# An attention stage whose projections, scores and value products yield more often to each other

## The chip, the cores and the metric

The program runs on one core of one Trainium2 chip. Five engines work side by side, each through its own list of instructions in a fixed order: TensorE (PE, matrix products; PEld is its weight load), VectorE (DVE), ScalarE (ACT), GpSimd (POOL) and SyncE (SP), which here issues nearly all of the transfers. The metric is device time in microseconds (us). The kernel before took 1922.65 us, the median of three runs (1921.36 to 1924.04).

## The reference

One step of a two-layer backbone runs over 128 context tokens and 512 latent tokens, 1024 wide. Layer 0 is softmax attention, layer 1 a gated delta rule; each is followed by an MLP of width 4096. The change touches layer 0's attention alone: 8 query heads of 128, 2 key/value heads. Cut to what it computes:

```python
proj = h @ w_in                                  # query, key and value columns
q, k = rms_norm(q, q_gain), rms_norm(k, k_gain)  # per head
q, k = axial_rope(q, ang), axial_rope(k, ang)    # latent tokens alone
s = einsum('bqkgd,bskd->bkgqs', q, k) * HEAD_DIM ** -0.5
o = einsum('bkgqs,bskd->bqkgd', softmax(s), v)   # latent queries see cached + latent keys
```

Context queries see context keys alone.

## The kernel before, in words

Activations lie as 128 features by 640 tokens, one tile per block of 128 features. Every fp32 matrix is split into a high and a low part (`split`: ScalarE copies the high part, another engine subtracts it), and one product is three matmuls (`mm3`: high by high, high by low, low by high).

A head passes three generators. `attn_proj` loads the head's weights (one transfer of 512 KB by SP; ScalarE makes the high part, GpSimd the low one), projects 320 tokens and then the other 320 (24 matmuls each, into one PSUM tile each; ScalarE copies the result and squares it), sums the squares by 10 short matmuls, and turns the query: four transfers on SP's queue fetch its quarters exchanged, GpSimd multiplies twice, VectorE adds, and the result is split again. `attn_scores` makes 24 score matmuls for four blocks of 128 latent queries and 3 for the context block; per block VectorE takes the maximum, ScalarE the exponential with its sum, VectorE the reciprocal, and GpSimd scales. `attn_values` transposes the four blocks' probabilities for one tile of keys (4 matmuls), ScalarE and VectorE split the result, and 3 matmuls add it to the output; this five times, then once for the context block.

What sets the order: `weave` runs generators in turns. It always advances the one whose next step has the smallest (steps done + 1) / weight. The loop at the end of `attention` runs eight rounds; round n weaves the value product of head n, the scores of head n+1 and the projection of head n+2. Before it, one weave holds keys, values and the query of head 0 (`attn_kv`, which ends with a projection of its own) beside eight loads of `w_mod` (`modulate`, two transfers of 512 KB each), and a second one the scores of head 0 beside the projection of head 1. The order that the generators give is a priority; a scheduler then lists each engine's instructions, and may put a ready one ahead of one that it takes to be waiting. An engine does not leave its list's order afterwards.

Buffers that matter: two PSUM tiles for the outputs of projection and value product together (`dense_ps`), two for scores (S), two for transposes and for the sums of squares (pt); three tiles for raw weights; three pairs of split weights, so that the pair of head n+5 takes the place of the pair of head n+2 when that projection is done.

After the last round PE runs the matmuls of the next `w_mod` slab and the output projection, whose loads wait for the raw tiles that these matmuls free.

## Time and profile before

| | |
|---|---|
| median of three runs | 1922.65 us |
| the profiled execution | 1918.51 us |
| its span, first to last instruction | 1916.7 us |
| TensorE busy | 1800.3 us, 94% |
| VectorE, ScalarE, GpSimd busy | 52%, 38%, 16% |
| mean granted TensorE clock | 0.979 |

The profiled execution lies 1.8 us above its span, and 4.1 us below the median of the runs. The span cut into 40 slices of 48 us puts the attention stage into slices 3 to 6 (about 60 to 277 us). A PE record covers a matmul from its start to its modelled end and overlaps the next one, so its busy share says less than the step from one start to the next; the chain of waits, which cuts time into pieces that do not overlap, gives these steps.

### The profile page before, as it was taken

How to read it: one execution, taken by the hardware profiler on the slowest of the kernel's cores; microseconds unless marked ns; L12 is line 12 of the kernel's file. 1: busy time of each engine (PE TensorE's matmuls, PEld its weight loads, DVE VectorE, ACT ScalarE, POOL GpSimd, SP SyncE). 2: the span in 40 equal slices, each digit the busy share in tenths (PEclk: the TensorE clock that was granted, in tenths of full speed). 3: DMA queues.
4: the chain of work that ended last, by engine and by line, in shares of the span. 5: the costliest groups of instructions: out<-in, count | busy, mean ns of one | idle time of the engine just before them, and what ended most of it. 6: DMA issues, size and time to landing. Idle time of an engine off the chain costs nothing.

```text
span 1916.7 us, 30963 instructions
## 1 busy us (share of the span) xinstructions
PE 1800.3 (94%) x12101; PEld 1675.9 (87%) x12101; DVE 987.6 (52%) x2272; ACT 734.8 (38%) x1550; POOL 309.4 (16%) x405
## 2 busy tenths in 40 slices
PE   6999999998989999999999999999599999999997
PEld 2778877977989999999989999787399999999997
DVE  5646663533454544455878776654455334343332
ACT  2445542431342423335646555533333223131331
POOL 2344221400100000042111112110142000000012
PEclk9999999999999999999999999999899999999999
DMA  7651137276876664324432234452822222222211
GB/s 279 219 162 34 34 115 220 68 236 214 263 209 197 197 190 142 102 81 157 126 101 87 77 89 130 155 163 94 269 74 82 72 78 78 77 72 73 78 44 56
DMA packets 286295, 248.83 MB, mean 130 GB/s; under 512 B 44127, under 2 KB 246262, under 8 KB 286150
## 3 DMA queue, kind: packets, MB, share of 16 engines
q1 hardware_dynamic: 266304, 207.85, 36.0%
q0 software_dynamic: 9136, 32.18, 4.8%
q10 hardware_dynamic: 10710, 6.83, 1.1%
q8 instruction: 95, 1.56, 0.3%
q14 instruction: 50, 0.41, 0.1%
HBM read 199.00 MB, written 45.20 MB: 127 GB/s over the span
## 4 chain that ended last, share of the span: by engine, by line
PE 67%; DVE 15%; DMA 10%; ACT 3%; issue 2%; POOL 1%; SPq 1%; POOLq 0%; ACTq 0%; DVEq 0%
PE dense L148 28%; PE pd L148 26%; DMA raw<-in_dn_w_in 3%; PE scan L148 3%; PE big L148 3%; DMA raw<-in_mlp_w 3%; DVE cv L141 2%; DVE wx L135 1%; DVE ptmp L135 1%; DMA raw<-in_w_mod 1%; PE mod L380 1%; PE big L151 1%; DVE ptri L1005 1%; DVE w L135 1%; PE pd L380 1%
## 5 line engine op out<-in xcount | busy, mean ns | idle before, releaser
L148 PE MATMUL pd<-h,w 128*128 128x320 f32 x2016 | 350.3, 319 | 7.3 <-ACT cv L138 3.7
L148 PE MATMUL dense<-a,wx 128*128 128x320 f32 x2238 | 340.8, 311 | 8.8 <-ACT wx L138 6.9
L148 PEld LDWEIGHTS dense<-a,wx 128*128 128x128 f32 x2238 | 332.7, 189 | 14.9 <-ACT wx L138 8.9
L148 PEld LDWEIGHTS pd<-h,w 128*128 128x128 f32 x2016 | 300.8, 190 | 22.4 <-issue 8.4
L148 PE MATMUL dense<-h,wx 128*128 128x320 f32 x1776 | 266.4, 309 | 5.4 <-DVE half L141 2.6
L148 PEld LDWEIGHTS dense<-h,wx 128*128 128x128 f32 x1776 | 261.5, 188 | 9.3 <-DVE half L141 4.2
L138 ACT ACTIVATE wx<-raw 128x1024 fp32r<-128x1024 f32 x132 | 139.5, 1058 | 306.7 <-PE dense L148 164.0
L135 DVE TENSOR_TENSOR wx<-raw,wx 128x1024 fp32r<-128x1024 f32 x127 | 157.3, 1240 | 153.6 <-ACT wx L138 153.4
L148 PE MATMUL pd<-a,wx 128*128 128x320 f32 x1284 | 199.2, 314 | 6.5 <-ACT a L138 4.7
L148 PEld LDWEIGHTS pd<-a,wx 128*128 128x128 f32 x1284 | 193.7, 191 | 8.3 <-ACT a L138 4.9
L148 PE MATMUL pd<-h,wx 128*128 128x320 f32 x1008 | 152.5, 309 | 2.8 <-ACT wx L138 1.4
L148 PEld LDWEIGHTS pd<-h,wx 128*128 128x128 f32 x1008 | 148.8, 188 | 4.5 <-DVE wx L135 1.9
L135 POOL TENSOR_TENSOR x<-x,half 128x320 f32<-128x320 f32 x48 | 50.2, 1045 | 581.3 <-ACT half L138 558.9
L141 DVE SCALAR_TENSOR_TENSOR x<-dense,c,x 128x320 f32<-128x320 f32 (+2 forms) x152 | 61.8, 435 | 156.9 <-PE dense L148 155.4
L135 DVE TENSOR_TENSOR w<-raw,w 128x1024 fp32r<-128x1024 f32 x45 | 57.2, 1271 | 117.1 <-ACT w L138 117.1
L138 ACT ACTIVATE w<-raw 128x1024 fp32r<-128x1024 f32 x54 | 57.2, 1060 | 145.2 <-DMA raw<-in_dn_w_in 122.5
L138 ACT ACTIVATE a<-half 128x320 fp32r<-128x320 f32 x128 | 60.3, 473 | 121.4 <-DVE half L141 121.3
L135 DVE TENSOR_TENSOR a<-half,a 128x320 fp32r<-128x320 f32 x128 | 62.8, 492 | 65.0 <-ACT a L138 64.7
L842 POOL DMA_DIRECT2D wd<-w x58 | 31.0, 535 | 333.7 <-ACT w L138 312.7
L141 DVE SCALAR_TENSOR_TENSOR cv<-cv,c,cv 128x644 f32<-128x644 f32 x84 | 77.7, 925 | 10.8 <-ACT cv L138 9.9
L141 DVE SCALAR_TENSOR_TENSOR x<-pd,c,x 128x192 f32<-128x192 f32 (+2 forms) x88 | 35.9, 437 | 79.5 <-PE pd L148 79.4
L138 ACT ACTIVATE half<-x 128x320 f32<-128x320 f32 x56 | 26.3, 470 | 106.8 <-DVE x L141 106.7
(281 smaller groups left out, 2481.8 us busy)
## 6 DMA issues: line engine op xcount, KB each, us to landing
raw<-in_mlp_w SPq DMA_DIRECT2D x128, 512.0 KB
raw<-in_w_mod SPq DMA_DIRECT2D x80, 512.0 KB
wd<-w POOLq DMA_DIRECT2D x58, 512.0 KB, 5.5
w<-wd SPq DMA_DIRECT2D x58, 512.0 KB
raw<-in_dn_w_in SPq DMA_DIRECT2D x32, 512.0 KB
raw<-in_attn_w_in SPq DMA_DIRECT2D x12, 512.0 KB
x<-xs SPq DMA_DIRECT2D x16, 320.0 KB
wide<-gd SPq DMA_DIRECT2D x16, 320.0 KB
```

The lines of the kernel that those rows point to most:

```text
L135: (eng or self.nc.vector).tensor_tensor(out=out, in0=in0, in1=in1, op=op)
L138: self.nc.scalar.activation(out=out, in_=in_, func=func, **kw)
L141: self.nc.vector.scalar_tensor_tensor(out=out, in0=in0, scalar=s, in1=in1, op0=op0, op1=op1)
L148: self.nc.tensor.matmul(out, l, r, start=first, stop=last)
L151: self.nc.tensor.transpose(out, in_, self.ident[:n, :n])
L380: nc.tensor.matmul(ps[32 * q : 32 * q + 32, :], self.cond[:, k, :], views[q], start=k == 0, stop=k == FT - 1, tile_position=(0, 32 * q),)
L842: self.nc.gpsimd.dma_start(out=d[i], in_=pair[i].bitcast(F32).rearrange("p k c -> p (k c)"))
L1005: nc.vector.tensor_reduce(out=t[:, BASE * i : BASE * i + i], in_=o, axis=AX.X, op=ALU.add)
```

## The change

The projection yields after each of the eight contraction tiles of a half (`dense_steps` in place of `dense_half`, the same matmuls); the scores yield between the two halves of the keys; the value product yields between the transposes of a tile and the matmuls of the tile before, and once before the context block's product. The weights of the weaves after the first are raised. The first weave keeps its weights 16 and 9, while `attn_kv`, which holds a projection, now has 30 steps in place of 16.

```diff
-            ps = self.dense_half(pair, h, half)
+            ps = yield from self.dense_steps(pair, h, half)
...
                 for hf in range(2):
                     self.mm3(s[:, hf, :], qp, tuple(t[:, hf * HALF : (hf + 1) * HALF] for t in self.keys[j]))
+                    if hf == 0:
+                        yield
...
             pend.append((kb, v, th, tl))
+            yield
             if kb:
                 values()
-            yield
+                yield
         values()
...
         self.split(pt[:, :P], th, tl)
+        yield
         po = self.dense_ps()
...
-            weave((self.attn_scores(0), 8), (self.attn_proj(h, 1), 3))
+            weave((self.attn_scores(0), 9), (self.attn_proj(h, 1), 17))
             for hd in range(HEADS):
-                parts = [(self.attn_values(hd), 6)]
+                parts = [(self.attn_values(hd), 12)]
                 if hd + 1 < HEADS:
-                    parts.append((self.attn_scores(hd + 1), 5))
+                    parts.append((self.attn_scores(hd + 1), 10))
                 if hd + 2 < HEADS:
-                    parts.append((self.attn_proj(h, hd + 2), 12))
+                    parts.append((self.attn_proj(h, hd + 2), 20))
```

Before, a round's projection has 3 steps of weight 12, so that all of it stands ahead of a quarter of the round. After, it has 17 steps of weight 20 beside 11 of the value product (weight 12) and 9 of the scores (weight 10): it ends at 0.85 of the round, among the last scores.

Three places of the built program show what the scheduler made of it. The number behind a name's last underscore tells instances apart.

First, PE around the projection of head 4, round 2. `pd_1752` is its first half in both; the second half is `pd_1789` before and `pd_1843` after. `S_...` are scores of head 3 (`S_1972` the context block), `pt_1831` and `pt_1937` the sums of squares, other `pt_...` transposed probabilities, `pd_1779` a value product, `pd_1984` the context block's one. Before, the end of the second half, which follows the first without a break:

```order
L148 MATMUL pd_1789<-h_402,w_1747 128x320
L148 MATMUL S_1816<-key_742,x_1605 128x320
L148 MATMUL S_1816<-key_741,x_1606 128x320
L148 MATMUL pt_1831<-c_84,a_1751 128x1 x2
L151 MATMUL pt_1866<-c_82,x_1577 128x128
L151 MATMUL pt_1866<-c_82,x_1639 128x128
L151 MATMUL pt_1866<-c_82,x_1666 128x128
L151 MATMUL pt_1866<-c_82,x_1693 128x128
L148 MATMUL pd_1779<-pv_1785,val_1079 128x512
L148 MATMUL pd_1779<-pv_1786,val_1079 128x512
L148 MATMUL pd_1779<-pv_1785,val_1080 128x512
L148 MATMUL S_1878<-key_741,x_1605 128x320
```

After, the start of the second half:

```order
L148 MATMUL S_1895<-key_741,x_1711 128x320
L148 MATMUL S_1895<-key_742,x_1711 128x320
L148 MATMUL S_1895<-key_741,x_1712 128x320
L148 MATMUL S_1895<-key_741,x_1711 128x320
L148 MATMUL S_1895<-key_742,x_1711 128x320
L148 MATMUL pd_1843<-h_388,w_1746 128x320
L148 MATMUL pd_1843<-h_389,w_1746 128x320
```

and its end, where the next round begins with `pt_2003`:

```order
L148 MATMUL pd_1843<-h_402,w_1747 128x320
L148 MATMUL pt_1937<-c_84,a_1751 128x1 x2
L148 MATMUL S_1972<-pkey_758,x_1711 128x128
L148 MATMUL S_1972<-pkey_759,x_1711 128x128
L148 MATMUL S_1972<-pkey_758,x_1712 128x128
L148 MATMUL pd_1984<-blk_1933,val_956 128x128
L148 MATMUL pd_1984<-blk_1934,val_956 128x128
L148 MATMUL pd_1984<-blk_1933,val_957 128x128
L151 MATMUL pt_2003<-c_82,x_1788 128x128
L151 MATMUL pt_2003<-c_82,x_1827 128x128
L151 MATMUL pt_2003<-c_82,x_1872 128x128
L148 MATMUL pt_1937<-c_84,a_1751 128x1 x3
```

The first half is woven among transposes and values; of the second half 21 matmuls stand in one piece, one score matmul later the last three. The second half has moved from the start of its round to the end, behind all four score blocks, and five sums of squares, the last three of which need the second half's squares, now have only small work between them and that half.

Second, ScalarE around the same projection; `w_2484` is the high part of head 7's weights, `x_1750` and `a_1751` the copy and the squares of the query. Before:

```order
L138 ACTIVATE x_1750<-pd_1752,c_93 128x320
L138 ACTIVATE a_1751<-pd_1752 128x320
L138 ACTIVATE w_2484<-raw_2482 128x1024
L138 ACTIVATE x_1750<-pd_1789,c_93 128x320
L138 ACTIVATE a_1751<-pd_1789 128x320
L138 ACTIVATE x_1823,sm_1825<-S_1816,mx_1824,rsy_1593 128x640
```

After:

```order
L138 ACTIVATE x_1788,sm_1790<-S_1766,mx_1789,rsy_1699 128x640
L138 ACTIVATE x_1827,sm_1829<-S_1805,mx_1828,rsy_1699 128x640
L138 ACTIVATE x_1750<-pd_1752,c_93 128x320
L138 ACTIVATE a_1751<-pd_1752 128x320
L138 ACTIVATE a_1927<-pd_1756 128x512
L138 ACTIVATE x_1872,sm_1874<-S_1856,mx_1873,rsy_1699 128x640
L138 ACTIVATE w_2484<-raw_2482 128x1024
L138 ACTIVATE x_1911,sm_1913<-S_1895,mx_1912,rsy_1699 128x640
L138 ACTIVATE x_1750<-pd_1843,c_93 128x320
L138 ACTIVATE a_1751<-pd_1843 128x320
```

The copy of the first half moved behind the exponentials of the first two score blocks; the copy of the second half behind the next weights' high part and the exponential of the fourth block.

Third, SP at the end of the first weave; `raw<-in_w_mod` are the loads of `modulate`, `dec<-x_799` the query of head 0 on its way through the rotation, `raw<-in_attn_w_in` the weights of heads 1 and 2. Before:

```order
L408 DMA raw_828<-in_w_mod 128x1024
L408 DMA raw_830<-in_w_mod 128x1024
L495 DMA dec_887<-x_799 32x512 x4
L408 DMA raw_898<-in_w_mod 128x1024
L408 DMA raw_900<-in_w_mod 128x1024
L408 DMA raw_938<-in_w_mod 128x1024
L408 DMA raw_940<-in_w_mod 128x1024
L408 DMA raw_1004<-in_w_mod 128x1024
L408 DMA raw_1006<-in_w_mod 128x1024
L187 DMA raw_1113<-in_attn_w_in 128x8x128
```

After:

```order
L408 DMA raw_805<-in_w_mod 128x1024
L408 DMA raw_807<-in_w_mod 128x1024
L408 DMA raw_819<-in_w_mod 128x1024
L408 DMA raw_821<-in_w_mod 128x1024
L408 DMA raw_833<-in_w_mod 128x1024
L408 DMA raw_835<-in_w_mod 128x1024
L408 DMA raw_847<-in_w_mod 128x1024
L408 DMA raw_849<-in_w_mod 128x1024
L495 DMA dec_920<-x_799 32x512 x4
L187 DMA raw_1083<-in_attn_w_in 128x8x128
```

The rotation of the query of head 0 moved behind the last six of these loads. No instruction is added or taken away on any engine.

## Rows read from the trace of the kernel before

**Rows 1.** The page: the span, and the engines' busy time with its share.
```profile
span 1916.7 us, 30963 instructions
PE 1800.3 (94%) x12101; PEld 1675.9 (87%) x12101; DVE 987.6 (52%) x2272; ACT 734.8 (38%) x1550; POOL 309.4 (16%) x405
```
**Rows 2.** Busy time of each engine in stretches of the attention stage, us from the span's start; the last three columns are granted clock, DMA share and GB/s. The cuts from 150.5 to 235 are the starts of the projections of heads 3 to 7.
```profile
150.50:171.90 21.40, 20.05 (x131) 18.32 (x131) 13.31 (x40) 11.92 (x28) 9.24 (x9) 1.00 0.13 38
171.90:193.40 21.50, 18.52 (x119) 16.58 (x118) 13.11 (x36) 10.90 (x24) 7.71 (x7) 1.00 0.14 37
193.40:216.40 23.00, 21.00 (x133) 18.73 (x134) 15.01 (x43) 12.17 (x31) 7.35 (x9) 1.00 0.12 36
216.40:235.00 18.60, 17.31 (x115) 15.84 (x113) 11.73 (x33) 9.90 (x21) 5.84 (x6) 1.00 0.15 42
```
**Rows 3.** The chain of waits in order of time, inside rounds: start, length, what. A projection half, a score block, sums of squares, a tile of transposes, a tile of values.
```profile
154.38 3.52 PE pd L148 x24
157.90 0.88 PE S L148 x6
...
160.08 0.58 PE pt L148 x6
...
272.48 0.44 PE pt L151 x4
...
274.36 0.70 PE pd L148 x3
```
**Rows 4.** What PE waited for between 111 and 277 us: total us, times, longest.
```profile
PE pd L148 <- DVE pv L135: 7.6, 12, 1.8
```
**Rows 5.** Groups of instructions between 150 and 235 us, shapes apart: busy us, mean ns of one, idle before.
```profile
L135 DVE TENSOR_TENSOR pv<-pt,pv 128x512 fp32r<-128x512 f32 x20 | 13.7, 682 | 9.3 <-ACT pv L138 9.3
L654 DVE TENSOR_REDUCE mx<-S 128x1 f32<-128x640 f32 x16 | 13.0, 814 | 11.2 <-PE S L148 11.2
L135 DVE TENSOR_TENSOR rst<-rsy 128x5 f32<-128x5 f32 x12 | 4.4, 368 | 0.1
L141 DVE SCALAR_TENSOR_TENSOR rsy<-rst,rsy 128x5 f32<-128x5 f32 x12 | 3.9, 324 | 0.0
L135 DVE TENSOR_TENSOR x<-dec,x 128x512 fp32r<-128x512 f32 x4 | 2.8, 711 | 0.0
L138 ACT ACTIVATE x<-S,mx,rsy 128x640 f32<-128x640 f32 x17 | 15.0, 883 | 9.3 <-DVE mx L145 6.2 <-DVE rst L135 1.6 <-DVE rsy L141 1.5
L138 ACT ACTIVATE w<-raw 128x1024 fp32r<-128x1024 f32 x4 | 4.2, 1060 | 8.3 <-PE pd L148 8.3
L138 ACT ACTIVATE x<-pd,c 128x320 f32<-128x320 f32 x8 | 4.2, 520 | 12.1 <-PE pd L148 12.1
L138 ACT ACTIVATE a<-pd 128x320 f32<-128x320 f32 x8 | 3.4, 430 | 0.0
L145 POOL TENSOR_SCALAR x<-x,sm 128x640 f32<-128x640 f32 x16 | 13.2, 826 | 28.6 <-DVE sm L657 18.3 <-DVE rst L135 2.9 <-DVE mx L145 2.6
L135 POOL TENSOR_TENSOR dec<-dec,a 128x512 f32<-128x512 f32 x4 | 5.1, 1284 | 2.1 <-DMA dec<-x 2.1
L135 POOL TENSOR_TENSOR w<-raw,w 128x1024 fp32r<-128x1024 f32 x2 | 4.8, 2385 | 13.3 <-ACT w L138 13.3
```
**Rows 6.** Instructions in order of time around one query's rotation: the copy on ACT, then the second multiplication on POOL, which waited for the transfers (in brackets, with the idle time ahead of it).
```profile
224.32 0.51 ACT L138 ACTIVATE x<-pd,c 128x320 f32<-128x320 f32 x1
...
228.88 1.30 POOL L135 TENSOR_TENSOR dec<-dec,a 128x512 f32<-128x512 f32 x1 [2.07 <-DMA dec<-x]
```
**Rows 7.** SP's transfers in order of time at the end of the first weave: start, length of the issue with its waits, what.
```profile
86.70 1.03 SPq L408 DMA_DIRECT2D raw<-in_w_mod  x2
91.33 2.42 SPq L495 DMA_DIRECT2D dec<-x  x4
93.85 14.28 SPq L408 DMA_DIRECT2D raw<-in_w_mod  x6
```
**Rows 8.** The chain of waits at the same place.
```profile
107.80 5.06 DMA raw<-in_w_mod
...
114.62 1.07 ACT w L138
...
115.75 2.40 POOL w L135
...
118.20 0.86 PE pd L148 x4
```
**Rows 9.** PE in order of time: the first sums of squares of head 1, which follow the last matmul of its projection, and the next stage's first matmuls, which follow the last of this one.
```profile
127.04 0.50 PE L148 MATMUL pt<-c,a 128*128 128x1 f32 x4
...
276.61 1.91 PE L380 MATMUL mod<-raw,c 128*32 128x512 f32 x10
```
**Rows 10.** The chain of waits in the last round: the last head's first tile on ACT and DVE.
```profile
269.22 0.60 ACT pv L138
...
269.85 0.70 DVE pv L135
```
**Rows 11.** Stretches of 10 us as in rows 2, around the one place of the stage where the clock fell.
```profile
180.00:190.00 10.00, 7.79 (x49) 6.71 (x49) 8.55 (x26) 5.76 (x13) 6.50 (x5) 1.00 0.30 79
250.00:260.00 10.00, 8.28 (x42) 7.05 (x43) 8.05 (x25) 5.67 (x14) 3.51 (x5) 0.83 0.21 70
```
**Rows 12.** SP's first transfers for the stage that follows.
```profile
277.70 11.04 SPq L408 DMA_DIRECT2D raw<-in_w_mod  x6
```

## The prediction, made before the changed kernel ran

> **What bounds the kernel now.** I read the page first: TensorE (PE) is busy for 94% of the span [rows 1], so a gain must come from its waits. Then the attention stage by rounds: from one projection's start to the next, 21.4, 21.5, 23.0 and 18.6 us, 21.1 on the mean [rows 2]. Then the chain of waits, for what PE needs at least per round. Its steps [rows 3] give 0.147 us per projection or score matmul (3.52 for 24, 0.88 for 6), 0.11 per transpose (0.44 for 4), 0.233 per value matmul (0.70 for 3) and 0.097 per sum of squares (0.58 for 6). A round holds 48 projection matmuls (7.05), 24 for scores (3.52), 21 transposes (2.31), 15 for values (3.50), 10 sums (0.97) and 6 small ones of the context block (0.66 at the transposes' rate): 18.0 us. So a round loses some 3.1 us, and the shortest one 0.6. The waits view puts most of it on VectorE's split of the transposed probabilities, 7.6 us in 12 waits [rows 4]. In turn VectorE's splits and maxima sat idle for 9.3 and 11.2 us in four rounds for what ScalarE and PE had not yet done [rows 5]: the projection is one block of 7 us that gives VectorE nothing, and what follows runs at the pace of VectorE and ScalarE. That speaks for weaving. What the new order gives is the question, since each engine keeps to its list.
>
> **The rounds after the change.** Let T be the instant when PE has issued the last matmul of a projection's second half; all times below are after T, for rounds 1 and 2, durations from [rows 3, 5] unless said otherwise.
>
> ScalarE has in its list, in this order, the next weights' high part (1.06; it overwrites the pair that this projection just left, so it cannot start before T), the exponential of the fourth score block (0.88), the copy of the query (0.52) and its squares (0.43): they end at 1.15, 2.0, 2.5 and 2.9. PE has in its list two sums, 3 score, 3 value and 3 transpose matmuls, 1.15 together; the next three sums need the squares. PE waits from 1.15 to 2.9: 1.75 lost. Before the change the next score block and a tile of transposes stood behind a projection, and nothing waited for its squares at once.
>
> GpSimd makes the low part of these weights (2.39, to 3.6) ahead of scaling the fourth block (0.83, to 4.45). PE does 3 sums and 3 projection matmuls (0.73, to 3.65) and then needs that block: 0.8 lost. From 4.45 it has 21 projection matmuls, 17 transposes and 10 of values, 7.3 us, to 11.75: here the weaving works, and VectorE's splits are covered.
>
> The query just projected is needed next. From its copy's end to GpSimd's second multiplication the trace has 4.05 us (224.83 to 228.88) [rows 6]. In the new order SP has a weight load ahead of these transfers whose raw tile is free only when GpSimd's split ends at 3.6, so they land at about 8.1; multiplication (1.28), addition on VectorE behind the third tile's split (to 10.5), high part on ScalarE behind the fourth tile's copy (11.7), low part on VectorE (0.71, 12.5). PE does what needs the high part alone, then finishes two score blocks at 13.2 and 13.8, and 5 matmuls more, to 14.75.
>
> The third block needs a score tile that the first one's exponential frees: VectorE takes two maxima (2 x 0.81) and scales, to 15.1, ScalarE's exponential ends at 16.05: 1.3 lost. The second half needs the PSUM tile of the first half, whose copy and squares stand behind both exponentials: 16.9 + 0.52 + 0.43 = 17.85; PE has just done the third and fourth block. So the second half is a filler for nothing, and its 25 matmuls end at 21.6. A round is 21.6: 18.0 of work and 3.6 of waits, where before had 21.1.
>
> Round 0 starts with more projection ahead of the sums and comes to 20.9. In rounds 3 to 5 the weights are the output projection's, split on VectorE (this kernel's two in the window are in no row here; I take as price half of GpSimd's 2.39): the 0.8 is gone, the query is ready at 11.1, and the round is 20.3. Six rounds: 20.9 + 2 x 21.6 + 3 x 20.3 = 125.0.
>
> **The last two heads.** With no projection left to fill, PE waits for the query of head 7, ready at 10.3; two blocks by 11.5, maxima, exponentials and the tile bound as above, all scores by 15.7, the last exponential at 18.8, scaled at 19.8 after a reciprocal. From the copy of the last head's first tile (269.22) [rows 10] to the stage's end (276.61) [rows 9] is 7.4 us; with a transpose and its copy's wait ahead, 27.5 after the last T. Together 152.5. Before, the same work, from the end of head 1's projection (127.04) to the end of the stage (276.61) [rows 9], took 149.6. Difference: +2.9.
>
> **The entry.** Before, PE waits 5.06 us for the last load of the first weave, then ScalarE (1.07) and GpSimd (2.40) split head 1's weights, and its projection starts at 118.2 [rows 8]. SP did not issue the loads evenly: from 87.7 to 93.8 it held the rotation of head 0 between them [rows 7]. After, eight loads go in one row, so I take the wait as gone, but the rotation goes last. By the steps above (4.05, 1.28, 0.7, then ScalarE behind PE's last key values, which I put at 112.3 as PE then works through) the query is ready at 113.75, and head 1's weights, next in both lists, at 114.8 + 2.4 = 117.2: 1.0 earlier. Bounds: the whole wait (-5.1) and, if the loads are as late as now and the rotation behind them, +0.5. I take -1.0, near to neither end, as the split of the weights is what both pass through.
>
> **What the trace does not show.** First, VectorE's short steps. The square root's iteration has means of 0.368 and 0.324 us for two of its three operations, on five columns [rows 5], three times each per round; in the new order they stand ahead of the first tile's split. Bounds per round: 0, or all of 3 x (0.368 + 0.324) = 2.1; I take 0.4, as PE has 0.7 in hand at 11.75 against 12.5: six rounds, +2.4. Second, PE's clock. It was 1.00 in a stretch where PE was busy for 7.79 of 10 us and 0.83 in one with 8.28 [rows 11]; 0.83 between levels of 1.2 and 2.4 GHz is 3.4 us at the lower one, a loss of 1.7 at most. The new order has 0.7 of work between 1.15 and 4.45 in two rounds, and waits of some 4 us in the last but one. Bounds: none, or a fall in each of the six rounds and two at the end, 13.6. I take one more than now, +1.7.
>
> The Trainium skill, page "TensorE: Matmul & The Clock Gate", section "A second HAM failure mode: psum-queue depth-cycling", tells of a kernel whose short idle spells between groups of matmuls made the clock swing and cost throughput. The trace agrees in one place of the stage and contradicts it in others with spells as long [rows 11]; by the rule, all eight falls would be paid, which is the third rival below.
>
> **The sum.** -1.0 + 2.9 + 2.4 + 1.7 = +6.0. What follows the stage moves with it: the next loads start when PE's first matmuls there free the raw tiles, at 277.7 [rows 12]. The profiled execution of before took 1918.5; after would be 1924.5 on the same terms. The median of before lies 4.1 above its profiled execution, so the forecast is 1922.65 + 6.0 = 1928.7. Measurement tells from no change what differs by more than 0.2%, 3.85 us.
>
> **Rivals.**
>
> Faster. The waits inside a round go, because the three generators fill each other's gaps: every round becomes like the shortest of before, 18.6 [rows 2]. Then six rounds take 111.6 in place of 125.0, and with entry and tail as above, and neither of the two unknown costs, the change is -1.0 + 111.6 + 27.5 - 149.6 = -11.5: 1911.1. For it: PE did have a round of 18.6. Against it: the second half is in one piece behind ScalarE, so it fills nothing. It decides from where the copy of the first half comes no later than PE's wait for the third block. A half-way house, 20 us a round, is -3.1.
>
> The Trainium skill, page "Perfetto Trace Analysis", section "Optimization Strategy", says that where the most contended engine changes over time, interleaving these regimes may help. The rounds do alternate so [rows 2]; by that rule this rival is the forecast, and the time is its 1911.1.
>
> No change. The order moves the waits without adding any: -1.0 + 2.9, with the unknown costs at zero, is +1.9: 1924.6. For it: three of four rounds of before lose as much as mine lose after. The change doing nothing of what its name says for the second half belongs here.
>
> Slower by much. The clock falls in each round, after the 1.75 or in the pair of waits up to 4.45, and what PE has to do from there, 7.3 us without a wait, is done at the lower level in part: -1.0 + 2.9 + 2.4 + 13.6 = +17.9, 1940.6. Against it: 1.00 in a stretch with 2.2 us idle [rows 11].
>
> **How the numbers follow.** My forecast with its neighbourhood, +4 to +12: 0.43. No change: 0.28. Faster: 0.22. Much slower: 0.07. So slower by over 0.2% 0.50, within 0.2% 0.28, faster by over 0.2% 0.22. The range is 1911 to 1938: it takes in the faster rival and leaves out most of the fourth; the forecast's own range is 1922 to 1936.
>
> **What would show each step.** Right: in rounds 1 and 2 of the new profile, from one second half's end to the next 21 to 22 us; PE idle for more than 1.5 us before the sums of squares, released by ScalarE; the fourth block's first transpose released by GpSimd; the second half in one block of 3.5 us. The stage ends 280 to 284 after the span's start. Wrong: rounds below 20 us, a second half that starts before the third score block, no wait for the squares, or a first weave that still has its wait of 5 us. An entry that gains 5 us in place of 1 would by itself bring the forecast to no change.

## The result and the profile after

| | before | after |
|---|---|---|
| median, side by side (4 runs each) | 1922.01 us (1915.85 to 1924.04) | 1942.84 us (1940.34 to 1947.36) |
| ratio, 95% interval | | 1.0115 (1.0092 to 1.0137) |
| span of the profiled execution | 1916.7 us | 1941.2 us |
| mean granted TensorE clock | 0.979 | 0.968 |

The change costs 20.8 us, where +6.0 was forecast: the direction was right, the time lies above the range (1911 to 1938). The first matmul of the next stage, 276.61 in [rows 9], in PE's order of time after the change:

```profile
299.76 0.64 PE L380 MATMUL mod<-raw,c 128*32 128x512 f32 x4
```

So 23.2 of the 24.5 us between the spans arise before it. The first transposes of the keys start at almost the same time in both traces (77.58 before, 77.50 after), so all of it arises behind them, in the rest of the first weave and in the rounds. Call T, as the prediction does, the instant when PE has issued the last matmul of a projection's second half. The windows of the stage after the change, cut at the end of head 1's projection, then at T of each round, then at the stage's end, follow; the columns are length, busy time of PE, PEld, DVE, ACT and POOL, granted clock, DMA share, GB/s:

```profile
131.40:153.40 22.00, 18.94 (x123) 16.95 (x122) 12.54 (x37) 11.15 (x24) 8.86 (x9) 1.00 0.21 59
153.40:176.10 22.70, 20.27 (x125) 18.76 (x125) 12.89 (x38) 11.20 (x25) 8.44 (x8) 0.92 0.13 36
176.10:199.30 23.20, 20.56 (x126) 18.82 (x125) 13.21 (x38) 11.19 (x25) 8.42 (x8) 0.93 0.13 35
199.30:222.50 23.20, 20.56 (x126) 18.71 (x125) 13.31 (x38) 11.20 (x25) 8.42 (x8) 0.93 0.13 35
222.50:243.80 21.30, 19.49 (x127) 17.19 (x126) 14.36 (x39) 11.19 (x25) 6.20 (x7) 1.00 0.14 38
243.80:266.70 22.90, 21.10 (x128) 18.68 (x126) 14.10 (x39) 11.19 (x25) 6.19 (x7) 0.93 0.13 35
266.70:299.80 33.10, 25.59 (x126) 19.29 (x127) 19.82 (x51) 15.39 (x35) 7.34 (x9) 0.85 0.32 104
```

The rounds took 21.3 to 23.2 us and the tail 33.1, where 20.3 to 21.6 and 27.5 were forecast. Five of the seven windows have a clock below 1.00. What PE waited for between 130 and 300 us (total us, times, longest) answers to [rows 4]:

```profile
PE S L148 <- ACT x L138: 9.4, 8, 2.0
PE pt L148 <- ACT a L138: 7.1, 6, 1.2
PE pt L151 <- POOL x L145: 3.1, 8, 0.8
...
PE pd L148 <- DVE pv L135: 0.7, 2, 0.3
```

The 7.6 us of waits for VectorE's splits are down to 0.7; in their place stand the three waits that the prediction names: for the third block's score tile (ScalarE's exponential), for the squares, for the fourth block (GpSimd). Behind the wait for the squares the clock falls. PE in order of time after the T of round 0, and the windows of 2 us there:

```profile
153.38 0.50 PE L148 MATMUL pt<-c,a 128*128 128x1 f32 x4
...
154.44 0.52 PE L151 MATMUL pt<-c,x 128*128 128x128 f32 x3
156.15 1.07 PE L148 MATMUL pt<-c,a 128*128 128x1 f32 x6 [1.19 <-ACT a L138]
157.08 1.15 PE L148 MATMUL pd<-h,w 128*128 128x320 f32 x3
```

```profile
152.00:154.00 2.00, 2.00 (x18) 2.00 (x16) 0.83 (x2) 0.57 (x1) 0.43 (x1) 1.00 0.00 0
154.00:156.00 2.00, 0.95 (x9) 0.71 (x8) 0.88 (x4) 2.00 (x6) 1.38 (x1) 1.00 0.00 0
156.00:158.00 2.00, 1.85 (x9) 1.84 (x10) 0.71 (x3) 0.90 (x5) 1.75 (x2) 0.64 0.03 8
158.00:160.00 2.00, 2.00 (x9) 1.93 (x8) 1.58 (x7) 0.60 (x1) 1.62 (x2) 0.50 0.89 266
```

Three projection matmuls, which step by 0.147 us each in [rows 3], now take about 0.9 us together (157.08 to 158.02). That is half the rate, at a clock of 0.50, the lower of its two levels, 1.2 GHz.

In the entry (the end of the first weave, up to the end of head 1's projection) SP issues all eight loads first and the rotation of head 0 last, as the order said; compare [rows 7]:

```profile
86.14 18.67 SPq L408 DMA_DIRECT2D raw<-in_w_mod  x8
104.91 2.42 SPq L495 DMA_DIRECT2D dec<-x  x4
```

PE still waits 1.86 us for the last load, and then 2.53 for head 0's query. In PE's order of time, before the change first, then after it (the last row is the first score of head 0):

```profile
112.91 1.05 PE L380 MATMUL S<-raw,c 128*32 128x512 f32 x4 [1.49 <-DMA raw<-in_w_mod]
```

```profile
111.83 1.59 PE L380 MATMUL S<-raw,c 128*32 128x512 f32 x4 [1.86 <-DMA raw<-in_w_mod]
...
119.16 1.97 PE L148 MATMUL S<-key,x 128*128 128x320 f32 x6 [2.53 <-ACT x L138]
```

### The profile page after: what moved, and what is told of

Same layout as the page of the kernel before. It is cut to its first block, busy times and chain, and to the rows that moved or that the text cites. A ratio compares the mean times of both kernels' runs of the same rounds, so it can differ in the third digit from the quotient of the medians.

```text
span 1941.2 us, 30973 instructions
## 1 busy us (share of the span) xinstructions
PE 1816.5 (94%) x12101; PEld 1686.4 (87%) x12101; DVE 986.0 (51%) x2272; ACT 732.8 (38%) x1550; POOL 307.3 (16%) x405
## 3 DMA queue, kind: packets, MB, share of 16 engines
q1 hardware_dynamic: 266304, 207.85, 35.6%
## 4 chain that ended last, share of the span: by engine, by line
PE 71%; DVE 12%; DMA 8%; ACT 3%; issue 3%; POOL 2%; SPq 1%; POOLq 0%; ACTq 0%; DVEq 0%
PE dense L148 30%; PE pd L148 27%; PE scan L148 3%; PE big L148 3%; DVE cv L141 2%; DMA raw<-in_mlp_w 2%; DVE ptmp L135 1%; PE mod L380 1%; PE S L148 1%; DMA raw<-in_dn_w_in 1%; PE big L151 1%; DVE wx L135 1%; PE pd L380 1%; DMA raw<-in_w_mod 1%; PE pt L151 1%
## 5 line engine op out<-in xcount | busy, mean ns | idle before, releaser
L148 PE MATMUL pd<-h,w 128*128 128x320 f32 x2016 | 360.8, 322 | 4.8 <-ACT cv L138 4.1
L148 PEld LDWEIGHTS pd<-h,w 128*128 128x128 f32 x2016 | 304.9, 192 | 20.0 <-issue 8.4
L138 ACT ACTIVATE wx<-raw 128x1024 fp32r<-128x1024 f32 x132 | 139.3, 1056 | 304.5 <-PE dense L148 163.0
L135 DVE TENSOR_TENSOR wx<-raw,wx 128x1024 fp32r<-128x1024 f32 x127 | 157.2, 1239 | 152.6 <-ACT wx L138 151.9
L148 PE MATMUL pd<-h,wx 128*128 128x320 f32 x1008 | 152.5, 309 | 1.8 <-ACT wx L138 0.9
L148 PEld LDWEIGHTS pd<-h,wx 128*128 128x128 f32 x1008 | 148.8, 188 | 3.4 <-DVE wx L135 1.4
L141 DVE SCALAR_TENSOR_TENSOR x<-dense,c,x 128x320 f32<-128x320 f32 (+2 forms) x152 | 61.8, 435 | 159.7 <-PE dense L148 158.3
```

The source lines that it names most:

```text
L135: (eng or self.nc.vector).tensor_tensor(out=out, in0=in0, in1=in1, op=op)
L138: self.nc.scalar.activation(out=out, in_=in_, func=func, **kw)
L141: self.nc.vector.scalar_tensor_tensor(out=out, in0=in0, scalar=s, in1=in1, op0=op0, op1=op1)
L148: self.nc.tensor.matmul(out, l, r, start=first, stop=last)
```

## The experiments

For every run, "stage" is the time from the end of head 1's projection to the first matmul of `mod` behind the stage (in e14, where scores of head 0 come behind that projection, from its first sums of squares), and "clock" the granted clock of that one window; both come from one profiled execution, the ratio from all runs. "At full clock" is the product of the two. It is an estimate of what the order alone would take, and a low one, since a low clock costs nothing while PE waits. Ratios whose intervals overlap are not told apart.

| run | ratio to before (95%) | stage, us | clock | at full clock |
|---|---|---|---|---|
| before | 1 | 149.6 | 0.99 | 148.1 |
| after | 1.0115 (1.0092 to 1.0137) | 168.4 | 0.93 | 156.6 |
| e6 scores' yield alone | 0.9996 (0.9976 to 1.0015) | 149.0 | 0.99 | 147.5 |
| e7 values' yields alone | 1.0055 (1.0035 to 1.0075) | 160.1 | 0.95 | 152.1 |
| e5 projection's steps alone | 1.0139 (1.0115 to 1.0163) | 176.7 | 0.89 | 157.3 |
| e21 entry alone | 1.0041 (1.0025 to 1.0057) | 156.6 | 0.95 | 148.8 |
| e4 scores and values | 1.0057 (1.0039 to 1.0076) | 160.1 | 0.94 | 150.5 |
| e1 all but the entry | 1.0111 (1.0071 to 1.0150) | 169.3 | 0.92 | 155.8 |
| e2 all, projection early | 1.0065 (1.0042 to 1.0087) | 158.2 | 0.99 | 156.6 |
| e3 after, PE kept busy | 1.0085 (1.0055 to 1.0114) | 161.4 | 0.98 | 158.2 |
| e11 same work elsewhere | 1.0169 (1.0143 to 1.0195) | 177.2 | 0.92 | 163.0 |
| e8 e1 and e3 and the tail | 1.0058 (1.0039 to 1.0077) | 158.3 | 1.00 | 158.3 |
| e10 e7, root a round later | 1.0003 (0.9989 to 1.0017) | 151.9 | 0.99 | 150.4 |
| e9 before, root a round later | 0.9989 (0.9969 to 1.0009) | 151.6 | 0.95 | 144.0 |
| e16 e9 and one yield | 0.9996 (0.9976 to 1.0017) | 148.4 | 0.99 | 146.9 |
| e12 e1, sums a round later | 1.0144 (1.0121 to 1.0168) | 176.4 | 0.90 | 158.8 |
| e14 e1, weights asked for later | 1.0095 (1.0067 to 1.0123) | 171.0 | 0.89 | 152.2 |

### One part at a time

**e6** takes the kernel before, with the yield between a score block's halves and the weights 9 and 10.

> The kernel before with the scores' yield between the halves of a block alone (weights 9 in the second weave and 10 in the rounds). Theory S (halves of a score block delay the maxima and exponentials, and with them the chain to the next block): most of the 10 us by which the run with coarse projections came later at the stage's end, 283 to 288, 1926 to 1932 us. Theory V (the value product's yields are what costs): stage's end within 2 us of 276.6 and time within 4 us of before.

Theory V holds so far: this part costs nothing that can be measured, and the stage ends at 276.6 as before.

**e7** takes the kernel before, with the three yields of `attn_values` and their weight of 12.

> The kernel before with the values' yields alone (weight 12 in the rounds). Theory V (a tile's transposes and the value product before it no longer stand together, so VectorE's split of a tile comes behind the root's short operations, which last 1.2 us each beside a GpSimd operation, and PE waits 2 us for it): stage's end at 283 to 288, 1926 to 1932 us. Theory S (the scores' halves cost): stage's end within 2 us of 276.6 and time within 4 us of before.

Theory V holds again: this part costs 0.55%. VectorE, then GpSimd, in order of time in round 1:

```profile
165.32 1.21 DVE L135 TENSOR_TENSOR rst<-rsy 128x5 f32<-128x5 f32 x1
...
168.44 1.22 DVE L135 TENSOR_TENSOR rst<-rsy 128x5 f32<-128x5 f32 x1
169.58 0.68 DVE L135 TENSOR_TENSOR pv<-pt,pv 128x512 fp32r<-128x512 f32 x1
```

```profile
165.21 1.29 POOL L135 TENSOR_TENSOR dec<-x,a 128x512 f32<-128x512 f32 x1
...
168.27 1.37 POOL L135 TENSOR_TENSOR dec<-dec,a 128x512 f32<-128x512 f32 x1
```

A VectorE operation on five columns, which takes 0.17 us at other times, ends within 0.03 us of the GpSimd operation that it meets. Two such stand ahead of the split that PE needs:

```profile
170.31 0.73 PE L148 MATMUL pd<-pv,val 128*128 128x512 f32 x2 [2.43 <-DVE pv L135]
```

These waits bring falls of the clock with them: the stage is 10.5 us longer than before's, of which 4.0 are left at full clock (152.1 less 148.1), and five of the six waits of over 1 us are followed by a fall.

**e5** takes the kernel before, with `dense_steps` for heads 1 to 7 and the weights 17 and 20.

> The kernel before with the projection's fine steps alone, for heads 1 to 7 (weights 17 in the second weave and 20 in the rounds; head 0's projection stays in two blocks, scores and values keep their coarse yields). Theory (the late second half alone makes the waits behind ScalarE and the clock's falls): PE waits over 1 us for the squares in most rounds, rounds of 21.5 to 23 us, stage's end at 288 to 296, 1931 to 1938 us. Rival (since the kernel with coarse projections and fine scores and values already lost 12 us, it is the latter that cost and the projection's steps are harmless): stage's end at 275 to 281, 1917 to 1924 us.

It costs 1.4%, more than even the theory's time: PE waits 8.1 us in 6 waits for the squares, and the clock is 0.89. So the late projection is the costliest part. The costs do not add: e5 and e7 alone come to 1.9% together, while e1, which holds both with the scores' yield, comes to 1.1%. Which part takes the cost of the other back, no run shows.

**e21** takes the kernel before, with `dense_steps` for head 0 alone.

> The kernel before with head 0's projection alone in fine steps, so that the first weave counts 30 steps and the rotation of head 0's query stands behind the last modulation loads, as in the changed kernel; everything after is as before. Theory (the late rotation costs what the profile shows): head 1's projection ends 52 to 54 us after the start of the keys' transposes in place of 49.5, and the whole is 2 to 5 us longer, 1.001 to 1.0025 of before. Rival (a later wait takes it up): 0.999 to 1.0005.

The theory holds, and the cost is above its bound: head 1's projection ends 52.4 us after the keys' first transposes (130.50 less 78.14), where it was 49.5 before, so 2.9 us later. The first round then takes 28.0 us, with falls of the clock in it: VectorE's low part of a query meets GpSimd's split of weights and takes 2.44 us, where it takes 0.69 before the change, PE waits 1.62 us for it, and the clock falls behind this wait (0.50 from 144 to 150 us). VectorE, GpSimd and PE:

```profile
140.82 2.44 DVE L135 TENSOR_TENSOR x<-dec,x 128x512 fp32r<-128x512 f32 x1 [1.48 <-ACT x L138]
```

```profile
140.34 2.36 POOL L135 TENSOR_TENSOR w<-raw,w 128x1024 fp32r<-128x1024 f32 x1 [2.42 <-ACT w L138]
```

```profile
143.31 1.04 PE L148 MATMUL S<-key,x 128*128 128x320 f32 x4 [1.62 <-DVE x L135]
```

In all the entry alone costs 0.41%, some 8 us.

**e4** has scores and values in fine steps and every projection in two blocks, with the weights 12, 10, 12 and 9, 3.

> The finer yields of scores and values alone: every projection in two blocks again, with weights 12 (values), 10 (scores), 12 (projection) in the rounds and 9 and 3 in the second weave, so the projection again goes first. Theory (the projection's fine steps are the whole loss, entry and rounds): the stage ends at 274 to 280 and the time is 1915 to 1926. Rival (the finer yields of scores and values cost too): the stage ends after 284 and the time is above 1930.

The rival holds (the stage ends at 287.2). With e6 and e7, the cost is the values'.

**e1** is the changed kernel with `dense_half` where `hd == 0`.

> The changed kernel, but head 0's projection (inside the first weave) is again in two blocks, so that the first weave counts 16 steps as before. Theory (the entry has a price of its own): the finer steps of head 0's projection put its rotation behind all loads of the modulation weights, so head 1's projection ends 4.3 us later than before (131.3 against 127.0); here it ends near 127 and the time is 4 to 6 us below the changed kernel's, 1937 to 1939. Rival (the entry only shifts what a later wait takes up anyway): the stage's end stays at 299 to 301 and the time within 2 us of 1942.8.

In the profile head 1's projection ends at 127.03 as before, and the stage at 296.3; the ratio is 1.0111 against 1.0115, no difference that these intervals can tell. So neither side holds, and the entry's share within the whole change stays open; e21 prices the entry by itself.

**e2** is the changed kernel with the projection's weight in the rounds 68 in place of 20.

> The changed kernel, but in the rounds the projection's weight is 68 in place of 20: its 17 fine steps are done in the first quarter of a round, as its three coarse ones were before. Scores and values keep their finer yields. Theory (the late second half makes the waits and, through them, the clock's falls): no wait before the sums of squares, at most two stretches of 10 us in the rounds below 0.95 of the clock, six rounds of 21 to 21.5 us in place of 22.6, tail of 27 to 29, time 1927 to 1933 (the entry's 4 us stay). Rival (the finer yields of scores and values are what costs): the rounds stay at 22 to 23 us and the time within 3 us of 1942.8.

The time, no waits for squares and a clock of 0.99 are the theory's; the rounds (up to 24.7 us) and the tail (33.2) are not: PE now waits 11.4 us for VectorE's splits (137 to 250), as in e7. Of its seven waits of over 1 us, up to 2.22, only one is followed by a fall, where e7 has five of six: the length of a wait does not decide by itself.

### Is it the clock?

**e3** is the changed kernel with transposes of the identity in `attn_proj`, for heads from 2:

```diff
         for b in range(NBLK):
+            if b == 2 and hd > 1:
+                for i in range(10):
+                    self.tr(ps[:, P : 2 * P], self.ident)
             self.mm(ps[:, b : b + 1], sq[:, b * P : (b + 1) * P], self.one_col)
+        if hd > 1:
+            for i in range(8):
+                self.tr(ps[:, P : 2 * P], self.ident)
```

> The changed kernel with more work for TensorE and nothing else: for heads 2 to 7 ten transposes of the identity into unused columns of the tile of the sums of squares, ahead of the last three sums (where PE waits 1.19 us), and eight behind them (where it waits 0.8 for the fourth block); they are read by nobody. 18 x 0.11 = 2.0 us more work per round, about as much as the two waits together. Theory A (the lower clock after these waits is most of the loss): the falls in 150:270 go, each round takes 21 to 22 us, the time falls by 6 to 12 us, to 1931 to 1937. Theory B (the waits themselves and what they delay are the loss; the clock is a bystander): the rounds stay as they are or grow by up to 0.5 us each, time 1942 to 1947.

**e11** is the changed kernel with the same 18 transposes into `pt[:, :P]`, in `attn_values` ahead of the third tile's first transpose (`kb == 2 and b == 1`).

> Control for the run with the transposes of the identity (1937.1 us): the changed kernel with the same 18 per round, in one row ahead of the third tile's transposes, in the middle of the fine steps where PE works without a wait, and none at the sums. Theory A (there they filled PE's waits and held up its clock): here the waits and the falls stay, and the 2 us per round are paid: stage's end at 305 to 313, 1948 to 1956 us. Theory B (any longer PE list shifts the other engines' work in its favour): stage's end at 290 to 297, 1934 to 1941 us.

Theory A holds in both, in e3 at the low end of its gain (5.8 us, with 6 to 12 expected). Against the changed kernel, work added at the sums leaves it 0.3% faster, where the two intervals still overlap a little, and the same work added where PE does not wait makes it 0.5% slower, with no overlap; nor do the intervals of the two runs overlap. In e3 the waits for squares fall from 6.0 us (131 to 267) to 0.6; in e11 they stay at 5.5, and the clock with them at 0.92.

**e8** has e1's and e3's edits, and for head 7 five transposes of the identity ahead of each of the first four of its probabilities.

> Three of the measures together: the changed kernel with head 0's projection in two blocks, the 18 transposes of the identity beside each sums of squares, and 5 more ahead of each of the first four transposes of head 7's probabilities (20 x 0.11 = 2.2 us more work), where PE waits 0.4 to 0.6 us each in the tail. If the terms add (entry 3 us, clock in the rounds 6, clock in the tail 2 to 4): no fall of the clock after 130, stage's end at 284 to 288, 1929 to 1933 us. If the extra work in the tail only delays it, 1934 to 1937. What is then left over the kernel before (about 10 us) is the order's own cost.

It is the only run whose clock is 1.00 throughout (one window over the stage):

```profile
125.90:284.20 158.30, 148.91 (x989) 133.31 (x988) 98.10 (x274) 82.13 (x183) 53.59 (x56) 1.00 0.19 56
```

With 128 matmuls more, 14 us at 0.11 each, the stage is 10 us shorter than after the change. The ratio is 1.0058, its interval clear of the changed kernel's: half the loss is back.

### What the values' yields cost

**e10** and **e9** move the reciprocal root from `attn_proj` to the start of `attn_scores`, in e7 and in the kernel before:

```diff
-        sc = self.rsqrt(sc)
...
         qh, ql, sc = self.q[hd]
+        sc = self.rsqrt(sc)
```

> The kernel with the values' yields alone (1932.4 us), and the root moved to the start of the head's scores. Theory (the values' yields cost because the root's short operations come ahead of VectorE's first splits, and PE waits 2.2 us in each of the first rounds): waits for these splits fall from 11.3 to under 6 us, stage's end at 276 to 281, 1919 to 1925 us. Rival (what costs is that the value product now comes behind other work in the list, whatever stands ahead of the split): stage's end 285 to 289, 1929 to 1934 us.

> The kernel before with one thing moved: the reciprocal root of a head's sums (ten operations on five columns on VectorE) is computed at the start of that head's scores, a round later, in place of right behind the projection. Theory (the root's operations, 1.2 us each where they meet GpSimd, stand ahead of VectorE's splits and cause PE's waits for them, 7.6 us in the stage): these waits halve, stage's end at 271 to 274, 1915 to 1918 us. Rival (they only fill VectorE's idle time, or hold the first maxima of the next scores instead): stage's end within 2 us of 276.6 or later, 1919 to 1926 us.

e10 bears the theory out: the 0.55% are gone, and the waits for splits are down from 11.3 to 6.3 us (under 6 was expected). e9 is the same as before within its interval, the rival's time, though its waits for these splits are gone (7.6 to 0.2). What took the gain shows in its PE order, and in windows of 2 us:

```profile
169.17 0.33 PE L148 MATMUL pd<-blk,val 128*128 128x128 f32 x1 [1.10 <-ACT blk L138]
```

```profile
166.00:168.00 2.00, 2.00 (x13) 1.49 (x11) 1.95 (x4) 1.26 (x3) 1.56 (x2) 1.00 0.00 0
168.00:170.00 2.00, 0.78 (x4) 0.57 (x4) 2.00 (x5) 0.79 (x2) 0.80 (x1) 0.99 0.00 0
170.00:172.00 2.00, 1.73 (x7) 1.23 (x6) 1.44 (x6) 1.20 (x2) 0.00 (x0) 0.50 0.04 8
172.00:174.00 2.00, 1.82 (x7) 1.82 (x8) 0.92 (x7) 0.87 (x5) 1.14 (x2) 0.50 0.00 0
174.00:176.00 2.00, 2.00 (x9) 2.00 (x9) 0.00 (x0) 0.00 (x0) 0.00 (x0) 0.50 0.00 0
176.00:178.00 2.00, 2.00 (x14) 1.99 (x13) 0.00 (x0) 0.00 (x0) 0.00 (x0) 0.80 0.00 0
```

A wait of 1.10 us is followed by 6.8 us at the lower level, of which half, 3.4, is lost. This happens in two rounds, which take 23.9 us, where the last two take 20.0.

**e16** is e9 with a `yield` ahead of the context block's product (values' weight 7).

> The kernel before with the root a round later, and one yield ahead of the context block's value product (weight of the values 7 for 6). With the root moved alone, four rounds took 20.0 to 21.4 us, but two took 23.9: PE waited 1.1 us for ScalarE's copy of that block and then had 6.8 us at the lower clock. Theory (that wait is what is left, and other work can stand in for it): no fall in the rounds, all six of 20 to 21.5 us, stage 4 to 8 us shorter than before's, 0.996 to 0.998 of before. Rival (the wait moves to the next copy or to VectorE's split of the values' result): one or two falls again, 0.999 to 1.002.

There is no fall in the rounds, which take 21.1 us three times and then 20.2, as the theory has it. But the tail is 34.7 us, with a fall in it, where it is 33.2 in the kernel before, the stage is 1.2 us shorter and not 4 to 8, and the ratio is 0.9996. Neither e9 nor e16 beats the kernel before by what can be measured.

### What the projection's steps cost

**e12** moves, on e1, sums and root from `attn_proj` to the start of `attn_scores`.

> The changed kernel with head 0's projection in two blocks (1939.7 us), and the sums of squares with their root moved to the start of the head's scores, so that PE has no matmul that waits for the squares right behind a projection. Theory A (that wait of 1.19 us per round, and the lower clock behind it, make up the rounds' loss): rounds of 20.5 to 21.5 us, at most two falls of the clock in 140:270, stage's end at 284 to 289, 1927 to 1932 us. Theory B (GpSimd's fourth block and ScalarE's third exponential hold PE anyway): the wait moves to the fourth block's transpose, rounds stay at 22 to 23, 1936 to 1941 us.

Theory B holds, and the time is worse than it said (1949.9 us, with 1936 to 1941 expected). The wait moved to the next projection, whose PSUM tile ScalarE's squares still read, and stayed in front of the fourth block (PE's waits, 127 to 300):

```profile
PE S L148 <- ACT x L138: 12.8, 10, 2.2
PE pd L148 <- ACT a L138: 6.5, 5, 1.3
PE pt L151 <- POOL x L145: 5.1, 6, 1.2
```

**e14** moves, on e1, the call of `pair` for the next head behind the second half's squares.

> The changed kernel with head 0's projection in two blocks (1.011 of before), and the request for the next head's weights (load, high part on ScalarE, low part on GpSimd) moved behind the copy and squares of a projection's second half. Theory A (ScalarE's order makes PE wait for the squares: 1.06 us for the weights' high part stand ahead of them): no wait over 0.3 us for squares in the rounds, at most three falls of the clock in 140:270, rounds of 21 to 22, stage 8 to 12 us shorter, 1.004 to 1.008 of before. Theory B (the weights come too late instead, or PE's other waits, for the third exponential and GpSimd's fourth block, bring the falls by themselves): rounds of 22.5 or more, 1.010 of before or above.

Neither theory is tested, as the edit did not do what it was made for. ScalarE in order of time shows the weights' part still ahead of the copy (191.70) and the squares (192.11); the scheduler's list has it there all the same.

```profile
189.87 1.06 ACT L138 ACTIVATE w<-raw 128x1024 fp32r<-128x1024 f32 x1 [2.33 <-PE pd L148]
...
191.70 0.51 ACT L138 ACTIVATE x<-pd,c 128x320 f32<-128x320 f32 x1
192.11 0.92 ACT L138 ACTIVATE a<-pd 128x320 f32<-128x320 f32 x2
```

**e19** and **e20** take that work away, from e1 and from the kernel before. Heads 3 to 7 use head 2's weights again, so five loads, five high parts and five low parts are left out together:

```diff
+        if hd < 3:
+            self.qp = self.q0 if hd == 0 else self.pair(...)
+        pair = self.qp
```

> The changed kernel with head 0's projection in two blocks, and with the query weights of heads 3 to 7 left out: head 2's are used again, so five loads, five high parts (ScalarE, 1.06 us) and five low parts (GpSimd, 2.39 us) are missing. On ScalarE the copy and squares then come right behind the projection, ahead of the fourth exponential. Theory A (the weights' parts make the waits at the sums and at the fourth block, and these the falls): both waits under 0.5 us, at most two falls of the clock in 130:270, rounds of 20 to 21.5 us, 1.000 to 1.005 of before. Theory B (the wait for the third exponential, 1.2 us, brings the falls alone): rounds of 22 to 23, 1.008 to 1.012.

> The kernel before with the same weights left out (heads 3 to 7 use head 2's). Both theories: it waits at other places (VectorE's splits), so little changes: 0.995 to 1.001 of before, rounds of 20.5 to 21.5 us.

The ratios are 1.0034 (1.0015 to 1.0053) for e19 and 0.9978 (0.9963 to 0.9994) for e20. So the same work is worth 0.2% in the old order and some 0.8% in the new one (e1 less e19). Theory A holds for the rounds. From 126 to 250 us e19 has no wait for squares left; the six rounds take 122.9 us, 135.3 in the changed kernel, between 19.6 and 21.5 each:

```profile
PE pt L151 <- POOL x L145: 4.2, 5, 1.0
PE S L148 <- ACT x L138: 1.2, 1, 1.2
```

One of its points failed: the wait for the fourth block did not shrink but is some 0.97 us in four rounds, as ScalarE now makes the fourth exponential behind copy and squares. e19's stage takes 158.5 us, 8.9 more than before's, and up to 6.8 of that is the clock in its tail, 35.6 us at 0.81:

```profile
249.70:285.30 35.60, 27.43 (x127) 20.85 (x125) 19.97 (x52) 15.44 (x37) 7.26 (x9) 0.81 0.30 96
```

## Why the prediction was wrong in size

**The rounds' order: the mechanism right, the size short.** At full clock (length by clock of the windows above), round 0 took 22.0 (20.9 forecast), rounds 1 and 2 20.9 and 21.6 (21.6), rounds 3 to 5 21.6, 21.3 and 21.3 (20.3), the tail 28.1 (27.5). The sum is 156.8, where 152.5 was forecast. ScalarE's row at T (weights, exponential, copy, squares; 153.43 to 156.09 in round 0) ended 2.7 after T (2.9 forecast), the second half ran in one piece at the end, and e2, e5 and e19 show the late second half and ScalarE's row to be what makes the waits for the squares. Two sizes were wrong. PE stopped 1.6 us after T (154.96) and not 1.15, as two sums are four matmuls in the trace; the prediction counts ten short matmuls in a round (0.97 us), but only two and then three in its steps. So the wait is 1.19 us and not 1.75. And the work of a round is not 18.0. Round 4 (222.5 to 243.8) ran at a clock of 1.00 and took 21.3 us with 1.8 of waits, so 19.5 of work:

```profile
225.28 0.83 PE L148 MATMUL pt<-c,a 128*128 128x1 f32 x6 [1.20 <-ACT a L138]
...
227.23 0.33 PE L151 MATMUL pt<-c,x 128*128 128x128 f32 x1 [0.28 <-POOL x L145]
...
237.80 0.74 PE L148 MATMUL pd<-pv,val 128*128 128x512 f32 x2 [0.33 <-DVE pv L135]
```

**VectorE's short steps: wrong.** The +2.4 are not there: the waits for splits are 0.7 us in all, and between 150 and 235 us the root's steps have means of 261 and 244 ns, below those of [rows 5]. The mechanism exists (e7, e10), but in the whole change another order of the engines avoids it.

**The clock: the step that failed.** "I take one more than now, +1.7". The windows give 168.4 less 156.8 at full clock, 11.6 us, against 1.5 before: +10, near the upper bound of 13.6 and some six times the term. e3, e11 and e8 show that it is the clock: more work shortens the stage where it fills the waits, and lengthens it where it does not. The argument against was one stretch with 2.2 us idle and no fall [rows 11]. That was the wrong lesson from one case: before the change the stage had three waits over 1 us (1.76, 1.11 and 1.12), one followed by a fall; after, it had twelve, six followed by one, and five of these six behind the wait for the squares. The count of long waits should have been carried into the price; by the rate of before, a third of twelve, that is four falls or 6.8 us.

The rival "slower by much" (1940.6, a chance of 0.07) named this mechanism and came within 2.2 us of the time. Some of that is luck, as its terms missed in both directions: its entry (-1.0) was 5.6 us too low, its order with the short steps (5.3) 3.4 too low, and its clock (13.6) some 3.5 too high. The Trainium skill's page "TensorE: Matmul & The Clock Gate", section "A second HAM failure mode: psum-queue depth-cycling", tells of short idle spells between groups of matmuls that make the clock swing. This trace agrees in six of its twelve waits of over 1 us, and not in the other six.

**The entry: wrong sign.** "I take -1.0"; head 1's projection ends 4.6 us later (131.62 against 127.04). The bound of +0.5 was too low as well. The 5.06 us of [rows 8] are the last load's part of the chain and not a wait of PE, which waited 1.49 us for it; after the change it waits 1.86, so there was less to gain than -5.1, and it is not gone. The step that failed is the query "ready at 113.75": the four transfers left SP from 104.91, GpSimd could multiply at 112.94 only, and ScalarE made the high part at 118.47, since the last key values stood ahead of it (to 116.6, with 112.3 forecast). The clock fell as well, to 0.78 and 0.88 in the two stretches from 110 to 130 us; in e21, where it is 1.00 there, the entry costs 2.9 us. Alone the entry costs 0.41% (e21); within the change its share could not be told (e1).

**The sum**, in stage time of the two profiled executions: the entry +4.6, the order 156.8 less 148.1 at full clock, +8.7 (forecast 2.9 + 2.4), and the clock +10. Together that is 23.3, where 23.2 was seen; the medians lie 20.8 apart. As the times at full clock are low estimates, the clock's share is at most what stands here and the order's at least.

Two things stay open: why one wait of 1.2 us is followed by a fall and the next is not, and what sets the tail, where e8's clock is 1.00 and 28.5 us remain.

## What to carry over

A finer weave moves waits between engines that keep their order: before yielding more often, look at which in-order engine stands between a filler's end and its next user, here ScalarE's weights and exponential ahead of the squares. Price each new TensorE wait of over 1 us not only with itself but also with a fall that may follow: here mostly some 3.4 us at half clock, 1.7 of it lost, behind anything from one wait in seven (e2) to five in six (e7). And undo a compound change part by part: here one part was free, one cost 0.55% for a reason that could be moved away, one 0.41% and one 1.4%, and the whole less than their sum.

## What the runs showed of the hardware

- A wait of 1.10 us behind a fully busy stretch was followed by 6.8 us at the clock's lower level (e9); waits of up to 2.22 us were followed by none in six cases of seven (e2).
- VectorE operations on two operands of five columns took 1.21 and 1.22 us beside GpSimd ones, ending with them, and 0.17 otherwise (e7); one on 512 columns took 2.44 us beside one, and 0.69 otherwise (e21). The Trainium skill's page "SBUF — State Buffer", section "SBUF: two separate sides", tells of a port pair that the two engines hold in turn for a whole instruction; the rows agree.
